# A planner that knows VectorE's delay between dependent neighbours, and convolution tiles one projection later, in a two-layer decoder trunk

## The chip, the core and the metric

The kernel runs on one NeuronCore of a Trainium2 chip. Its engines have their own instruction queues and meet by semaphores: TensorE (PE; its weight loads are PEld), VectorE (DVE), ScalarE (ACT), GpSimd (POOL) and SyncE (SP, which here only issues DMAs). The metric is the device time of one execution in microseconds, lower is better. Before the change it is 1433.64 us, the median of three runs from 1433.3 to 1433.87.

## What is computed

A causal decoder trunk of two layers on a sequence of 512 tokens with 1024 channels. Layer 0 mixes tokens by a gated linear recurrence and pooling, layer 1 by a conformer convolution module; behind either come cross-attention to 256 memory tokens and a gated feed-forward with a short convolution. The change touches the conformer's code and the scheduler of all. The conformer:

```python
def conformer_conv(x, norm, w1, b1, dw_w, dw_b, ln_g, ln_b, w2, b2):
    h = rms_norm(x, norm) @ w1 + b1
    h = jax.nn.glu(h, axis=-1)
    h = causal_dwconv(h, dw_w, dw_b)
    h = jax.nn.silu(layer_norm(h, ln_g, ln_b))
    return h @ w2 + b2

def layer(x, mem, ...):
    x = x + (mixer_ab(x, ...) if layer % 2 == 0 else conformer_conv(x, ...))
    x = x + cross_attn(x, mem, ...)
    return x + conv_ffn(x, ...)
```

All is float32. The depthwise convolution has 31 taps for each channel.

## The kernel before

Channels lie on the 128 partitions, tokens along the free dimension; the 1024 channels are 8 chunks of 128 x 512. A float32 product is made of three matmuls of rounded halves: the operand is split into a high part (ScalarE copies it to fp32r) and a low part (VectorE, or GpSimd, subtracts), and high x high, high x low, low x high are summed in PSUM (`mm3`). So one projection of a chunk is 8 x 3 = 24 matmuls of 512 columns, and every weight needs a ScalarE copy and a subtraction (in the profile wr<-wf and wr<-wf,wr).

**Who sets the order.** The kernel's code doesn't issue instructions. Every call makes a node in a `Recorder`, which notes what the node reads and writes; `run` (line 498 issues everything, so L498 is the line of nearly all rows) puts the nodes out in the order of `plan`. `plan` is a list scheduler: it walks through a modelled time; each engine, when it is free, takes the ready node that is due first (`late` computes the due times backwards from the end), but TensorE takes the ready node that was recorded first, up to 60 nodes ahead of its head (`PE_WINDOW`). The costs of nodes are a table in `cost` (line 271), DMAs among them. A node that depends on one of the same engine was ready as soon as that one's time had passed (`hop`, line 454); one on another engine 0.04 us after the end plus a latency. Buffers of PSUM are given out in order: five "mm", two "aux", one "stat". Each engine then runs its queue strictly in the order planned.

**The conformer** (`conformer`, line 1340). For each chunk c there are two projections, the gate (`gate`, followed by ScalarE's sigmoid) and the value (`gated`, where VectorE writes h = (value + bias) x sigmoid into one of three padded buffers). Of the 31 taps of the convolution, TensorE does the first 8 for chunks 0 to 6 and all for chunk 7 (`PE_GROUPS`): four DMAs on SP copy 32 channels each into four tiles with four shifts stacked (`stacked`, in the profile actf<-h), and `conv_pe` multiplies them by small tap matrices, in groups of four tiles that each fill 32 of the 128 output partitions (aux<-actf,wf; the shapes end in 512, 508 and so on). `conv` does the other taps of chunks 0 to 6: four on ScalarE and GpSimd, and 19 on VectorE, each of which adds to the aux tile what the tap makes of h (aux<-h,par,aux), so each depends on the one before it of the same chunk. `merge` then adds both parts and the bias on VectorE (actf<-aux,par,actf) and frees the aux buffer. After chunks 3 and 7 the sums over channels for the mean are taken on TensorE (`quarters`, stat<-actf,onesf); mean, variance and scale follow, and with the normalised chunks the output projections (pw2). To have matmuls for TensorE meanwhile, parts of the next cross-attention's work are recorded between: `mem.keys(n)` (24 matmuls of 256 columns each) and `mem.values` (48 matmuls of 512 each). The loop (line 1439) records for each c: gate projection of c+1, tiles of c, value projection of c+1, taps of c; behind the last chunk's tiles come the loads for the values.

Of the kernel before, what the change touches and what calls it, by code (L numbers as in the profile page):

```python
# [21 lines left out]
C = D // P  # L22
# [15 lines left out]
N_POOL = [4] * 7 + [0]  # L38
LAG = 5
PLAIN = 3  # L40

KE = 4
# [140 lines left out]
class Node:  # L183

    def __init__(self, index, eng):
        self.index, self.eng, self.calls, self.us, self.tail = index, eng, [], 0.0, 0.0
        self.table, self.port, self.lat = None, False, 0.0
        self.before, self.after = set(), set()
        self.start = self.end = None
# [11 lines left out]
class Recorder:  # L201
# [5 lines left out]
    WIRE = 0.83 / (256 * 1024)  # L207
    LAND = {"SP": 1.9, "ACT": 1.9, "POOL": 2.3}

    def __init__(self, tc):  # L210
# [36 lines left out]
    def touch(self, node, v, write):  # L247
        t = v.tile
        lo, hi, mask, _ = v.region()
        if t.psum:  # L250
            lo, hi, mask = 0, 127, 1
        if not t.nodes:
            self.tiles.append(t)
        if not t.nodes or t.nodes[-1] is not node:
            t.nodes.append(node)

        def meets(e):
            return e[0] <= hi and lo <= e[1] and e[2] & mask

        for e in t.writes + (t.reads if write else []):  # L260
            if meets(e) and e[3] is not node:
                node.before.add(e[3])
        if write:
            keep = lambda e: not (lo <= e[0] and e[1] <= hi and (e[2] & mask) == e[2])
            t.writes = [e for e in t.writes if keep(e)]
            t.reads = [e for e in t.reads if keep(e)]
            t.writes.append((lo, hi, mask, node))
        else:
            t.reads.append((lo, hi, mask, node))

    def cost(self, node, eng, method, args, how, reads):
        out = args[0]
        n = int(np.prod((reads[0] if not isinstance(out, View) else out).shape[1:]))
        if method == "dma_start":
            src = out if isinstance(out, View) else reads[0]
            node.tail += self.WIRE * 4 * n * src.shape[0] * (1.9 if "accum_op" in how else 1)
            window = any(k[0] == "window" for k in src.steps) or any(k[0] == "window" for r in reads for k in r.steps)
            node.us += 0.65 if window else {"SP": 0.42, "ACT": 0.42, "POOL": 0.6}[eng]
            return
        if eng == "PE":  # L280
# [3 lines left out]
            elif out.shape[0] == 32:  # L284
                node.us += 0.875 / 4
            else:
# [32 lines left out]
    def plan(self):  # L319
# [19 lines left out]
        def late(extra):  # L339
            for o in reversed(nodes):  # L340
                due = end if o.ideal is None else o.ideal + o.us
                for a in list(o.after) + extra.get(o, []):
                    due = min(due, a.due - self.HOP - o.lat - (o.tail + self.LAND[o.eng] + self.SAFE if o.tail else 0.0))
                o.due = due - 1.15 * o.us
# [51 lines left out]
        while done < len(nodes):  # L396
# [11 lines left out]
            for e, r in ready.items():  # L408
# [4 lines left out]
                for i, (_, _, o) in enumerate(r):  # L413
# [39 lines left out]
                    heapq.heappush(soon, (o.end, o.index, "end", o))  # L453
                    hop = lambda a: now + us if a.eng == o.eng and not o.tail else o.end + self.HOP
                    for a, at in [(a, hop(a)) for a in o.after] + [(a, now) for a in opens.get(o, [])]:
# [54 lines left out]
def trunk(ctx: ExitStack, tc: tile.TileContext, I: dict, out_t: bass.AP, out: bass.AP):  # L510
# [132 lines left out]
    class Norm:  # L643
        due = None
# [695 lines left out]
    def conformer(norm, nxt, mem, parked):  # L1340
# [97 lines left out]
        mu = stat_ps()  # L1438
        for c in range(C):
            if c < C - 1:  # L1440
                b = gate(c + 1, project(w[0], c + 1, norm.x))
                spread(c + 1)
            else:
                mem.keys(KE)
            conv_pe(c)
            if c < C - 1:
                gated(c + 1, b, project(w[1], c + 1, norm.x))
                if c < C - 2:
                    w = pieces(c + 2)
            else:  # L1450
                mem.eng = G
                ready = [mem.piece(i, park=True) for i in range(4)] + [mem.piece(i) for i in range(4, 8)]
            conv(c)
        merge(*pend.pop())
# [18 lines left out]
        mem.values(1, ready[4:])  # L1473
        for n in range(KE + 1, C):
            mem.keys(n)
# [128 lines left out]
```

## Time and profile before

| what | before |
|---|---|
| median of the runs | 1433.64 us (1433.3 to 1433.87) |
| the profiled execution's own time | 1433.83 us |
| its span, first to last instruction | 1432.0 us |
| PE busy | 1421.8 us |
| DVE busy | 1223.8 us, 1874 instructions |
| ACT busy | 853.2 us |
| POOL busy | 185.3 us |
| granted TensorE clock | 1.000 |

The profile is of one execution. Rows name an instruction by its engine, the line, and out<-in by the program's tiles (mm, aux, stat are PSUM; act, actf, wf, wr, tmp, h lie in SBUF). "x16" is a count. A time in brackets is the engine's idle time before the row and what ended it. The conformer stands between 735 and 925 us of the span, the two feed-forwards at about 350 to 735 and 1050 to 1425.

### The profile page before, as it was taken

To read this page: it belongs to the slowest core of one execution; us is meant where nothing else is said; L and a number is where in the kernel's file an instruction comes from. 1 tells how busy PE (TensorE), PEld (TensorE's weight loads), DVE (VectorE), ACT (ScalarE), POOL (GpSimd) and SP (SyncE) were. 2 spreads that over 40 slices of the span, in tenths; PEclk is the share of its full clock that TensorE was granted. 3 is DMA by queue.
4 is the path that set the end of the run, shared out by engine and by line. 5 is a ranking of instruction groups with operands and counts; after the bars stand their busy time and mean duration, and the time that the engine had idled before them with its cause. 6 is when DMAs were issued, how large, how long until landed. Compare 5 with 4: busy or idle time off the path is not lost. (4 is left out here: it accounts for less than half of the span.)

```text
span 1432.0 us, 20240 instructions
## 1 busy us (share of the span) xinstructions
PE 1421.8 (99%) x7512; PEld 1199.9 (84%) x7512; DVE 1223.8 (85%) x1874; ACT 853.2 (60%) x1298; POOL 185.3 (13%) x196
## 2 busy tenths in 40 slices
PE   9999999999999999999999999999999999999998
PEld 8888888888988888888886676888898888888888
DVE  8986964758999999999967996776699999999996
ACT  8578854446866566656643436654577665666654
POOL 0000000001111010110006663300011111011000
PEclk9999999999999999999999999999999999999999
DMA  9332322228877786886515572322688777787821
GB/s 349 104 103 74 123 96 90 76 86 224 234 205 209 208 215 188 216 211 178 166 57 136 134 230 75 118 84 79 175 230 213 205 192 221 205 222 181 216 90 60
DMA packets 75988, 231.91 MB, mean 162 GB/s; under 512 B 8561, under 2 KB 10609, under 8 KB 75889
## 3 DMA queue, kind: packets, MB, share of 16 engines
q1 hardware_dynamic: 61488, 192.20, 40.7%
q0 software_dynamic: 13824, 37.75, 15.6%
q8 instruction: 59, 0.97, 0.3%
q10 hardware_dynamic: 576, 0.67, 0.1%
q14 instruction: 41, 0.33, 0.1%
HBM read 207.52 MB, written 2.10 MB: 146 GB/s over the span
## 5 line engine op out<-in xcount | busy, mean ns | idle before, releaser
L498 PE MATMUL mm<-act,wr 128*128 128x512 f32 (+1 forms) x4599 | 987.3, 368 | 1.7 <-ACT tmp L498 1.0
L498 PEld LDWEIGHTS mm<-act,wr 128*128 128x128 f32 x4599 | 802.1, 188 | 155.2 <-issue 5.8
L498 ACT ACTIVATE wr<-wf 128x1024 fp32r<-128x1024 f32 x295 | 308.4, 1053 | 116.8 <-PE mm L498 27.0
L498 DVE TENSOR_TENSOR wr<-wf,wr 128x1024 fp32r<-128x1024 f32 x272 | 329.4, 1219 | 37.3 <-ACT wr L498 18.7
L498 PE MATMUL aux<-act,wr 128*128 128x512 f32 (+1 forms) x1509 | 293.7, 337 | 0.1
L498 PEld LDWEIGHTS aux<-act,wr 128*128 128x128 f32 x1509 | 232.6, 190 | 28.8 <-ACT tmp L498 0.5
L498 ACT ACTIVATE tmp<-aux 128x512 f32<-128x512 f32 (+1 forms) x189 | 107.5, 571 | 94.8 <-PE aux L498 93.6
L498 DVE TENSOR_TENSOR tmp<-tmp,tmp 128x512 f32<-128x512 f32 (+1 forms) x151 | 99.4, 658 | 10.1 <-ACT tmp L498 6.3
L498 POOL DMA_DIRECT2D wf<-in_wup x48 | 42.7, 889 | 500.9 <-ACT act L498 275.9
L498 DVE TENSOR_TENSOR x<-x,mm 128x512 f32<-128x512 f32 (+1 forms) x126 | 81.5, 648 | 22.3 <-PE mm L498 21.6
L498 DVE SCALAR_TENSOR_TENSOR aux<-h,par,aux 128x497 f32<-128x497 f32 (+18 forms) x133 | 93.1, 731 | 4.7 <-PE aux L498 2.1
L498 POOL DMA_DIRECT2D wf<-wf x48 | 41.5, 864 | 382.0 <-PE mm L498 129.7
L498 ACT ACTIVATE act<-tmp 128x512 fp32r<-128x512 f32 (+1 forms) x85 | 52.9, 627 | 59.5 <-DVE tmp L498 59.4
L498 ACT ACTIVATE act<-actf 128x512 fp32r<-128x512 f32 (+1 forms) x136 | 70.0, 536 | 28.4 <-DVE actf L498 26.4
L498 PE MATMUL aux<-act,act 128*128 128x256 f32 (+1 forms) x456 | 84.4, 327 | 0.0
L498 PEld LDWEIGHTS aux<-act,act 128*128 128x128 f32 x456 | 73.7, 189 | 11.4 <-ACT tmp L498 0.5
L498 DVE TENSOR_TENSOR act<-actf,act 128x512 fp32r<-128x512 f32 (+1 forms) x136 | 76.0, 583 | 1.7 <-ACT act L498 1.5
L498 DVE SCALAR_TENSOR_TENSOR tmp<-h,par,tmp 128x512 f32<-128x512 f32 x96 | 72.0, 750 | 5.3 <-ACT tmp L498 2.7
L498 ACT ACTIVATE tmp<-h,par 128x512 f32<-128x512 f32 (+3 forms) x69 | 52.6, 782 | 31.2 <-DVE h L498 30.9
L498 POOL TENSOR_TENSOR wr<-wf,wr 128x1024 fp32r<-128x1024 f32 x23 | 55.1, 2406 | 91.2 <-PE mm L498 42.2
L498 DVE TENSOR_TENSOR tmp<-mm,tmp 128x512 f32<-128x512 f32 x84 | 57.1, 685 | 6.4 <-PE mm L498 6.1
L498 DVE TENSOR_TENSOR act<-tmp,act 128x512 fp32r<-128x512 f32 (+1 forms) x85 | 57.6, 682 | 0.4 <-ACT act L498 0.2
(150 smaller groups left out, 1067.2 us busy)
## 6 DMA issues: line engine op xcount, KB each, us to landing
wf<-in_wup SPq DMA_DIRECT2D x144, 512.0 KB, 4.8
wf<-in_wup POOLq DMA_DIRECT2D x48, 512.0 KB, 5.7
wf<-in_wdown SPq DMA_DIRECT2D x48, 512.0 KB, 5.3
actf<-in_wup SPq DMA_DIRECT2D x48, 256.0 KB, 6.3
wf<-wf POOLq DMA_DIRECT2D x48, 256.0 KB, 6.0
wf<-in_pw SPq DMA_DIRECT2D x24, 512.0 KB, 4.0
wf<-in_win SPq DMA_DIRECT2D x20, 512.0 KB, 3.6
wf<-in_wk SPq DMA_DIRECT2D x16, 512.0 KB, 5.9
```

The lines of the kernel that those rows point to most:

```text
L498: getattr(eng, method)(*[real(a) for a in args], **{k: real(v) for k, v in how.items()})
```

## The change

It has three parts. The planner gets a delay (`DRAIN`): a node that reads what the node before it on VectorE (or ScalarE) wrote is ready 0.12 us (0.2 us) after that one's time, in the forward walk and in the due times. Costs are changed: a copy with stacked shifts takes SP 0.8 us rather than 0.65, and its bytes count twice; a convolution tile is 0.225 us, and 0.06 more in a first group. And the conformer's loop is written in half steps, one projection each, with the tiles and taps of a chunk `AFTER` = 2 half steps behind its own projection, which is behind the next chunk's whole projection; at the end one more block of keys (`mem.keys`) is recorded ahead of the last tiles.

```diff
+AFTER = 2
...
-        self.before, self.after = set(), set()
+        self.before, self.after, self.feeds = set(), set(), set()
...
+    DRAIN = {"DVE": 0.12, "ACT": 0.2}
...
                 node.before.add(e[3])
+                if not write:
+                    e[3].feeds.add(node)
...
-            node.us += 0.65 if window else {"SP": 0.42, "ACT": 0.42, "POOL": 0.6}[eng]
+            node.tail *= 2.0 if window else 1.0
+            node.us += 0.8 if window else {"SP": 0.42, "ACT": 0.42, "POOL": 0.6}[eng]
...
-                node.us += 0.875 / 4
+                node.us += 0.9 / 4 + (0.06 if how["start"] else 0.0)
...
-                    due = min(due, a.due - self.HOP - o.lat - (o.tail + self.LAND[o.eng] + self.SAFE if o.tail else 0.0))
+                    if a.eng == o.eng and not o.tail:
+                        due = min(due, a.due - self.DRAIN.get(o.eng, 0.0))
+                    else:
+                        due = min(due, a.due - self.HOP - o.lat - (o.tail + self.LAND[o.eng] + self.SAFE if o.tail else 0.0))
...
-                    hop = lambda a: now + us if a.eng == o.eng and not o.tail else o.end + self.HOP
+                    drain = self.DRAIN.get(o.eng, 0.0)
+                    same = lambda a: now + us + (drain if a in o.feeds else 0.0)
+                    hop = lambda a: same(a) if a.eng == o.eng and not o.tail else o.end + self.HOP
...
-        for c in range(C):
-            if c < C - 1:
-                b = gate(c + 1, project(w[0], c + 1, norm.x))
-                spread(c + 1)
+        for i in range(2 * C - 2 + AFTER):
+            c = i // 2 + 1
+            if i >= 2 * C - 2:
+                mem.keys(KE + i - 2 * C + 2)
+            elif i % 2 == 0:
+                b = gate(c, project(w[0], c, norm.x))
+                spread(c)
             else:
-                mem.keys(KE)
-            conv_pe(c)
-            if c < C - 1:
-                gated(c + 1, b, project(w[1], c + 1, norm.x))
-                if c < C - 2:
-                    w = pieces(c + 2)
-            else:
+                gated(c, b, project(w[1], c, norm.x))
+                if c < C - 1:
+                    w = pieces(c + 1)
+            if i == 2 * C - 2:
                 mem.eng = G
-                ready = [mem.piece(i, park=True) for i in range(4)] + [mem.piece(i) for i in range(4, 8)]
-            conv(c)
+                ready = [mem.piece(k, park=True) for k in range(4)] + [mem.piece(k) for k in range(4, 8)]
+            c = i + 1 - AFTER
+            if c >= 0 and c % 2 == 0:
+                conv_pe(c // 2)
+                conv(c // 2)
...
-        for n in range(KE + 1, C):
+        for n in range(KE + AFTER, C):
             mem.keys(n)
```

What this does to the queues is shown at three places. First TensorE around the tiles of chunk 1. Before (mm_7514 is the value projection of chunk 2, aux_7545 the convolution of chunk 1):

```order
L498 MATMUL mm_7514<-act_7308,wr_7116 128x512
L498 MATMUL mm_7514<-act_7298,wr_7346 128x512
L498 MATMUL aux_7545<-actf_7472,wf_7365 32x512
L498 MATMUL aux_7545<-actf_7482,wf_7365 32x512
L498 MATMUL aux_7545<-actf_7491,wf_7365 32x512
L498 MATMUL aux_7545<-actf_7499,wf_7365 32x512
L498 MATMUL aux_7545<-actf_7472,wf_7365 32x508
L498 MATMUL aux_7545<-actf_7482,wf_7365 32x508
L498 MATMUL aux_7545<-actf_7491,wf_7365 32x508
L498 MATMUL aux_7545<-actf_7499,wf_7365 32x508
L498 MATMUL mm_7514<-act_7310,wr_7116 128x512
L498 MATMUL mm_7514<-act_7320,wr_7116 128x512
```

And TensorE at the same place now (mm_7507 is the value projection of chunk 2, mm_7568 the gate of chunk 3):

```order
L508 MATMUL mm_7507<-act_7331,wr_7114 128x512
L508 MATMUL mm_7507<-act_7324,wr_7128 128x512
L508 MATMUL aux_7545<-actf_7450,wf_7354 32x512
L508 MATMUL aux_7545<-actf_7460,wf_7354 32x512
L508 MATMUL aux_7545<-actf_7469,wf_7354 32x512
L508 MATMUL aux_7545<-actf_7476,wf_7354 32x512
L508 MATMUL aux_7545<-actf_7450,wf_7354 32x508
L508 MATMUL aux_7545<-actf_7460,wf_7354 32x508
L508 MATMUL aux_7545<-actf_7469,wf_7354 32x508
L508 MATMUL aux_7545<-actf_7476,wf_7354 32x508
L508 MATMUL mm_7568<-act_7233,wr_7348 128x512
L508 MATMUL mm_7568<-act_7243,wr_7348 128x512
```

Before, the 8 tiles stood between matmul 18 and 19 of that projection; now all 24 are ahead of them.

Second VectorE at the taps of chunks 0 and 1. Before (aux_7435 and h_112 are chunk 0, aux_7545 and h_114 chunk 1, h_116 is the new h of chunk 2):

```order
L498 SCALAR_TENSOR_TENSOR aux_7435<-h_112,par,aux_7435 128x483
L498 SCALAR_TENSOR_TENSOR aux_7435<-h_112,par,aux_7435 128x482
L498 SCALAR_TENSOR_TENSOR aux_7545<-h_114,par,aux_7545 128x500
L498 SCALAR_TENSOR_TENSOR aux_7545<-h_114,par,aux_7545 128x499
L498 SCALAR_TENSOR_TENSOR h_116<-mm_7514,par,tmp_7518 128x512
L498 SCALAR_TENSOR_TENSOR aux_7545<-h_114,par,aux_7545 128x498
L498 SCALAR_TENSOR_TENSOR aux_7545<-h_114,par,aux_7545 128x497
L498 SCALAR_TENSOR_TENSOR aux_7545<-h_114,par,aux_7545 128x496
L498 SCALAR_TENSOR_TENSOR actf_7163<-aux_7435,par,actf_7163 128x512
L498 SCALAR_TENSOR_TENSOR aux_7545<-h_114,par,aux_7545 128x495
```

VectorE at these taps now (aux_7478 is chunk 0):

```order
L508 SCALAR_TENSOR_TENSOR h_116<-mm_7507,par,tmp_7513 128x512
L508 SCALAR_TENSOR_TENSOR aux_7478<-h_112,par,aux_7478 128x490
L508 SCALAR_TENSOR_TENSOR aux_7478<-h_112,par,aux_7478 128x489
L508 SCALAR_TENSOR_TENSOR aux_7545<-h_114,par,aux_7545 128x500
L508 SCALAR_TENSOR_TENSOR aux_7478<-h_112,par,aux_7478 128x488
L508 SCALAR_TENSOR_TENSOR aux_7545<-h_114,par,aux_7545 128x499
L508 SCALAR_TENSOR_TENSOR aux_7478<-h_112,par,aux_7478 128x487
L508 SCALAR_TENSOR_TENSOR aux_7545<-h_114,par,aux_7545 128x498
L508 SCALAR_TENSOR_TENSOR aux_7478<-h_112,par,aux_7478 128x486
L508 SCALAR_TENSOR_TENSOR aux_7545<-h_114,par,aux_7545 128x497
```

Taps of one chunk stood behind each other; now the taps of two chunks alternate, and so it goes on to chunk 6.

Third VectorE behind the LayerNorm's scale (aux_8500, then aux_8503), where the first normalised chunk (act) and the weights of the first three output projections (wr<-wf,wr) are made. Before:

```order
L498 TENSOR_TENSOR actf_7291<-actf_7291,aux_8500 128x512
L498 TENSOR_TENSOR actf_7480<-actf_7480,aux_8500 128x512
L498 SCALAR_TENSOR_TENSOR wr_8545<-mm_8160,rt,wr_8496 128x512
L498 SCALAR_TENSOR_TENSOR wr_8545<-mm_8340,rt,wr_8496 128x512
L498 TENSOR_TENSOR wr_8564<-wf_8472,wr_8540 128x1024
L498 TENSOR_TENSOR act_8576<-actf_8519,act_8553 128x512
L498 TENSOR_TENSOR act_8578<-actf_8559,act_8569 128x512
L498 TENSOR_TENSOR wr_8588<-wf_8503,wr_8574 128x1024
L498 TENSOR_TENSOR wr_8597<-wf_8510,wr_8590 128x1024
```

VectorE at that place now:

```order
L508 TENSOR_TENSOR actf_7495<-actf_7495,aux_8503 128x512
L508 TENSOR_TENSOR actf_7629<-actf_7629,aux_8503 128x512
L508 TENSOR_TENSOR actf_7631<-actf_7631,aux_8503 128x512
L508 TENSOR_TENSOR wr_8563<-wf_8445,wr_8505 128x1024
L508 SCALAR_TENSOR_TENSOR wr_8573<-mm_8237,rt,wr_8552 128x512
L508 TENSOR_TENSOR act_8577<-actf_8519,act_8558 128x512
L508 TENSOR_TENSOR wr_8583<-wf_8461,wr_8540 128x1024
L508 TENSOR_TENSOR wr_8595<-wf_8483,wr_8568 128x1024
```

Five chunks were scaled ahead of the first operand, and two value parts; now seven chunks and one value part. On TensorE the first three output projections ran two channel chunks of the first weight, then of the second and third; now they go through the three weights for one channel chunk after the other.

## The prediction

> **What bounds the kernel now.** The page comes first:
>
> ```profile
> span 1432.0 us, 20240 instructions
> PE 1421.8 (99%) x7512; PEld 1199.9 (84%) x7512; DVE 1223.8 (85%) x1874; ACT 853.2 (60%) x1298; POOL 185.3 (13%) x196
> ```
>
> TensorE is busy 1421.8 of 1432.0 us, and the change takes no matmul away. So only time in which TensorE waits can be won. The waits of PE, all of them:
>
> ```profile
> PE aux L498 <- DMA actf<-h: 1.6, 3, 1.0
> PE stat L498 <- POOL onesf L573: 1.0, 1, 1.0
> PE mm L498 <- ACT tmp L498: 1.0, 2, 0.5
> PE mm L498 <- DVE act L498: 0.6, 1, 0.6
> ```
>
> Read alone they leave little: 4.2 us, of which 1.6 belong to the convolution tiles (aux<-actf,wf), which wait for their shifted copies (actf<-h). But a matmul's end is modelled, so a wait can hide inside "busy". Starts are safer. Below, TensorE in seven stretches: each from the first tile of one chunk's convolution (chunks 0 to 6) to the next matmul that is no convolution tile, which starts where the stretch ends; the columns are the stretch, its length, the busy time of the tiles, clock, DMA share, GB/s.
>
> ```profile
> 759.14:761.35 2.21, 2.21 (x16) 1.00 0.00 0
> 772.47:774.32 1.85, 1.85 (x16) 1.00 0.09 38
> 784.10:789.38 5.28, 4.04 (x16) 1.00 0.79 258
> 801.85:803.70 1.85, 1.85 (x16) 1.00 0.13 53
> 814.84:818.06 3.22, 2.88 (x16) 1.00 0.59 188
> 828.71:830.53 1.82, 1.82 (x20) 1.00 0.93 369
> 843.01:845.68 2.67, 2.67 (x16) 1.00 0.87 324
> ```
>
> The same 8 tiles (two records each) take 1.85 us when nothing holds them, and 5.28, 3.22, 2.67 and 2.21 in chunks 2, 4, 6 and 0. The sum is 18.90 us against 7 x 1.85 = 12.95: **5.95 us** of waiting, not 1.6. [...]
>
> What the tiles of chunk 2 wait for stands in the DMA queue, TensorE and VectorE's own order:
>
> ```profile
> 777.89 0.75 DVE L498 SCALAR_TENSOR_TENSOR h<-mm,par,tmp 128x512 f32<-128x512 f32 x1
> 778.67 4.26 SPq L498 DMA_DIRECT2D actf<-h  x4
> 787.55 1.90 PE L498 MATMUL aux<-actf,wf 128*32 128x512 f32 x10 [0.98 <-DMA actf<-h]
> ```
>
> VectorE writes h at 777.89, four copies are issued over 4.26 us, and the last tile can go at 787.55: h to tiles is **9.7 us**. VectorE itself is the second bound of this stage, and in the middle of the feed-forward:
>
> ```profile
> 100.00:150.00 50.00, 50.00 (x222) 41.41 (x221) 38.31 (x57) 44.40 (x59) 0.23 (x2) 1.00 0.26 85
> 500.00:550.00 50.00, 49.52 (x259) 42.12 (x258) 48.28 (x72) 31.31 (x45) 6.10 (x7) 1.00 0.76 211
> 800.00:850.00 50.00, 49.67 (x244) 33.90 (x243) 49.01 (x74) 18.08 (x27) 30.49 (x22) 1.00 0.60 174
> ```
>
> After the stretch and its length come PE, PEld and DVE busy. From 800 to 850 VectorE is busy 49.01 of 50 us. The first row also gives the price of a 128x512 matmul that nothing disturbs: 50/222 = 0.225 us.
>
> **Part 1: tiles behind the next chunk's whole projection.** Before, 36 matmuls (chunk 2) or 42 (chunk 4) stand between the end of a chunk's projection and its tiles, which cut into the next chunk's second projection (the first order piece). Now 48 to 60 stand there, and the tiles of the chunk before: at least 48 x 0.225 + 1.85 = 12.7 us. Needed are the 9.7 us from h to tiles, which leaves 3.0 for an h that VectorE writes late; in the new order a merge and a tap stand right ahead of h, 1.3 us. So I count all 5.95 us as gone. If the cover fails (SP's queue holds the copies behind a weight load that waits for a free buffer), a chunk waits again, by 0.4 to 3.4 us as above. Chunk 7's tiles stood in two pieces, now in one:
>
> ```profile
> 789.38:801.85 12.47, 12.47 (x56) 1.00 0.59 161
> 827.82:828.71 0.89, 0.89 (x10) 1.00 0.95 348
> 858.15:860.84 2.69, 2.69 (x25) 1.00 0.28 105
> 864.03:868.29 4.26, 4.26 (x41) 1.00 0.00 0
> ```
>
> The first row holds 54 projection matmuls by the order: 12.47 - 54 x 0.225 = 0.3 us is what a switch between the two kinds costs. One switch fewer is 0 to 0.3; I take **0.2**.
>
> **Part 2: who is late next.** With two aux buffers, chunk c's tiles need chunk c-2 merged on VectorE. So VectorE's total has to fit. VectorE now:
>
> ```profile
> 764.33 13.66 DVE L498 SCALAR_TENSOR_TENSOR aux<-h,par,aux 128x497 f32<-128x497 f32 x18
> 793.36 3.90 DVE L498 SCALAR_TENSOR_TENSOR aux<-h,par,aux 128x484 f32<-128x484 f32 x6
> 797.16 0.75 DVE L498 SCALAR_TENSOR_TENSOR actf<-aux,par,actf 128x512 f32<-128x512 f32 x1
> ```
>
> 18 taps that each add to what the one before wrote: (777.89 - 764.33)/18 = **0.753 us** a tap. The six at 793.36 alternate between two chunks by the order: (797.16 - 793.36)/6 = **0.633**. The changed order has 21 dependent neighbours among its 133 taps, where there were 73. From chunk 0's first tap to chunk 6's merge that makes 112 x 0.633 + 21 x 0.753 + 13 x 0.66 (six h, seven merges) + 2.3 (one weight split, three key steps) = 97.6 us. TensorE's work beside it, from the end of chunk 0's tiles to the second sum for the mean: 321 matmuls x 0.225 + two key blocks at 3.1 + 6 x 1.85 + 6.95 (chunk 7) + 0.9 (first sum) + 8 switches x 0.3 = 99.8 us. They fit by 2 us, so the chain isn't slower than TensorE; but in the order a merge stands only two rows ahead of the next h, and the tiles that need it follow directly behind the projection that h needs. Seven such hand-overs at 0 to 0.2 us: **+0.5**, bounds 0 and 1.5. As it was, the last merge was early:
>
> ```profile
> 865.63 0.75 DVE L498 SCALAR_TENSOR_TENSOR actf<-aux,par,actf 128x512 f32<-128x512 f32 x1
> 874.14 2.48 DVE L498 TENSOR_TENSOR actf<-actf,aux 128x512 f32<-128x512 f32 x4 [6.51 <-PE aux L498]
> ```
>
> **Part 3: the LayerNorm and the first output projections.** Behind the spread scale, TensorE has 45 key matmuls to do and then needs the first normalised chunk and three weights:
>
> ```profile
> 888.47 5.95 PE L498 MATMUL mm<-wr,wr 128*128 128x256 f32 x45
> 894.26 0.39 PE L498 MATMUL mm<-act,wr 128*128 128x512 f32 x1
> 895.26 2.93 PE L498 MATMUL mm<-act,wr 128*128 128x512 f32 x11 [0.61 <-DVE act L498]
> 889.07 3.08 DVE L498 TENSOR_TENSOR actf<-actf,aux 128x512 f32<-128x512 f32 x5 [0.79 <-PE aux L498]
> 892.07 1.40 DVE L498 SCALAR_TENSOR_TENSOR wr<-mm,rt,wr 128x512 fp32r<-128x512 f32 x2
> 893.39 1.22 DVE L498 TENSOR_TENSOR wr<-wf,wr 128x1024 fp32r<-128x1024 f32 x1
> 894.52 1.29 DVE L498 TENSOR_TENSOR act<-actf,act 128x512 fp32r<-128x512 f32 x2
> ...
> 897.22 1.23 DVE L498 TENSOR_TENSOR wr<-wf,wr 128x1024 fp32r<-128x1024 f32 x1 [0.28 <-issue]
> ```
>
> Before, VectorE scales 5 chunks, splits two values and a weight, then the first operand (act), then the two other weights. Now it scales 7 at 0.60, one weight at 1.13, one value at 0.66, the operand at 0.62, two weights at 1.13. From 889.07 this puts the operand's end at 895.7 (was 895.2) and the third weight's at 898.0. TensorE starts at 894.26 and has 8 matmuls (1.8 us) to do before that third weight, where it had 14 (3.2) before 898.4 (the row at 897.22): it waits 2.0 us where it waited 1.0. So **+1.0**, bounds 0 (the scale arrives earlier against TensorE) and +2.2 (one key block, 3.1 us, has moved ahead of the chain, and 9 value matmuls, 2.0 us, behind its start, so that the cover shrinks by another 1.1).
>
> **Part 4: VectorE's order elsewhere.** Dependent neighbours on VectorE fall from 405 to 145 in the whole program, and at 0.12 us each it is relieved of some 30 us. That buys little, since TensorE hardly waits there; the two waits for ACT are
>
> ```profile
> 526.20 0.74 PE L498 MATMUL mm<-act,wr 128*128 128x512 f32 x2 [0.48 <-ACT tmp L498]
> ```
>
> and its twin in the second layer. TensorE's rows outside the conformer move by groups of 3 to 20. I take 0, bounds -1.0 (both waits go) and +3.0 (six such waits are added).
>
> **Sum**, against the profiled execution's own 1433.83 us (its span of 1432.0 and 1.8 around it): -5.95 - 0.2 + 0.5 + 1.0 + 0 = -4.65, 1429.2 us. The median of the runs is 0.2 below that execution, so **1429.0**. With all bounds on the good side -7.25, with all on the bad side about +0.8 (the copies covered, all else at its worst).
>
> **Rivals.**
> 1. *The waits only change their name.* The hand-overs of part 2 cost 1.5, part 3 2.2, part 4 another 1: -5.95 - 0.2 + 4.7 = -1.5, so 1432. For it: VectorE and TensorE are within 2 us over 100. Against it: the sums say that they fit. The same time comes if the copies are late again in one chunk (3.4 of the 5.95 was chunk 2 alone).
> 2. *Slower: alternating gains nothing, and VectorE becomes the bound.* If each tap took 0.753 whatever its neighbour, the 97.6 us would be 111.0, 11 above TensorE's work, and with only two buffers TensorE waits all of it: 1429 - 0.5 + 11.2 = 1440. It decides from 0.70 us a tap, where 112 x 0.067 uses up the 2 us of room and the gain. Against it: the six alternating taps at 0.633. [...]
> 3. *Slower: fillers.* A scheduler that sees the delay puts a 1.13 us weight split where 0.12 us of waiting stood, 49 times between the sum that reads PSUM and the one that needs it (66 such neighbours before, 17 after). If each held a buffer so long that TensorE waited the 0.48 of the row above, it would cost 23 us: 1452. It decides from 10 places. Against it: VectorE has no less total time than before, and TensorE's buffers (five mm, two aux) hid all but two such delays.
> 4. *The change doesn't do what it says*: excluded by the order, where both moves can be read.
>
> **How the numbers follow.** Forecast 0.76 (1426.4 to 1430.8), rival 1 0.16, rival 2 0.03, rival 3 0.05. Faster by over 0.2% (2.9 us, about what a measurement of this kernel can tell from none) is the forecast's case, below 1430.8; rival 1 is within 0.2%; 2 and 3 are slower. The range from 1426.0, just under all the good bounds together, to 1433.0, most of rival 1, leaves out the slow ones and the last part of rival 1.
>
> **What would show it.** In the profile after: the seven stretches of tiles at 1.85 each (part 1); no PE wait for DMA actf<-h; tap pitch 0.633 in alternation and VectorE's stretch from first tap to last merge near 98 us (part 2); a PE wait of 1.5 to 2.5 us in the first three output projections (part 3); still at most a few waits of 0.5 for ACT in the feed-forwards (part 4). Waits of PE for VectorE ahead of aux tiles beyond 2 us together, or more than four waits in the feed-forwards, would make it wrong.

## The result, and the profile after

The changed kernel takes 1423.95 us (median of five runs, 1423.58 to 1426.22) against 1433.6 before: a ratio of 0.9936, 95% interval 0.9922 to 0.995. The forecast was 1429.0 in a range from 1426.0 to 1433.0; the kernel gained 9.7 us where 4.6 were forecast. The profiled execution took 1423.58 us.

The page of the changed kernel, its span and first row:

```profile
span 1421.8 us, 20232 instructions
PE 1413.4 (99%) x7512; PEld 1198.6 (84%) x7512; DVE 1202.0 (85%) x1874; ACT 847.0 (60%) x1299; POOL 185.0 (13%) x196
```

VectorE does the same 1874 instructions in 21.8 us less. TensorE does the same 7512 matmuls and its busy time is 8.4 us less, at an unchanged clock: so most of what was won had been counted as "busy".

Where the time went shows best when both executions are cut at the same matmuls, the 1700th, 3400th, 4800th, 5300th and 7200th in TensorE's order. Each row is a stretch between two of them: its ends, its length, then PE, PEld, DVE, ACT and POOL busy with the number of instructions, clock, DMA share, GB/s. They are the start (layer 0's mixer and attention), the first feed-forward, the conformer and the second feed-forward; the second attention between the last two, 99.6 us in both, and the end behind them, the same in both, are left out. Before:

```profile
1.03:351.22 350.19, 350.19 (x1701) 296.46 (x1701) 260.71 (x410) 221.38 (x342) 8.49 (x33) 1.00 0.40 130
351.22:659.29 308.07, 307.48 (x1701) 266.86 (x1700) 300.28 (x451) 198.52 (x292) 35.58 (x41) 1.00 0.79 212
659.29:934.00 274.71, 272.53 (x1402) 209.57 (x1401) 225.56 (x332) 139.11 (x202) 99.05 (x68) 1.00 0.43 132
...
1033.57:1381.79 348.22, 347.62 (x1902) 300.87 (x1901) 337.46 (x510) 224.14 (x332) 39.04 (x45) 1.00 0.77 207
```

And after:

```profile
1.03:350.51 349.48, 349.32 (x1701) 295.20 (x1701) 258.63 (x410) 221.56 (x343) 7.51 (x32) 1.00 0.40 130
350.51:656.51 306.00, 306.00 (x1701) 267.25 (x1700) 294.88 (x451) 195.78 (x291) 36.34 (x42) 1.00 0.81 214
656.51:926.08 269.57, 268.09 (x1403) 208.74 (x1401) 217.96 (x332) 138.21 (x202) 99.13 (x68) 1.00 0.44 134
...
1025.66:1371.63 345.97, 345.97 (x1902) 301.21 (x1900) 331.78 (x510) 221.62 (x331) 38.93 (x45) 1.00 0.78 208
```

The conformer's stretch is 5.1 us shorter (274.71 to 269.57; the forecast was 4.65). The feed-forwards are 2.07 and 2.25 shorter and the start 0.7; there the forecast was 0. Together that is 10.2 us between these two executions; the medians differ by 9.7. In the first feed-forward PE was "busy" 307.48 us for work that now takes 306.00, so a wait of 1.5 us stood inside the busy column, and only 0.6 outside it.

One such place in the first feed-forward before. The columns are start, duration, and a group of TensorE's matmuls; the bracket is the idle time that the profile shows:

```profile
493.32 1.57 PE L498 MATMUL aux<-act,wr 128*128 128x256 f32 x8
494.95 1.31 PE L498 MATMUL mm<-act,wr 128*128 128x512 f32 x5
...
524.14 1.57 PE L498 MATMUL aux<-act,wr 128*128 128x256 f32 x8
526.20 1.57 PE L498 MATMUL mm<-act,wr 128*128 128x512 f32 x7 [0.48 <-ACT tmp L498]
```

The same two places after:

```profile
491.62 1.57 PE L508 MATMUL aux<-act,wr 128*128 128x256 f32 x8
493.04 1.55 PE L508 MATMUL mm<-act,wr 128*128 128x512 f32 x8
...
522.12 1.57 PE L508 MATMUL aux<-act,wr 128*128 128x256 f32 x8
523.53 1.55 PE L508 MATMUL mm<-act,wr 128*128 128x512 f32 x8
```

From the start of the same eight matmuls to the next group it was 1.63 and 2.06 us, and is 1.42 and 1.41. The first loss, 0.21, has no bracket at all; the second is 0.65 where the bracket says 0.48.

The waits of PE that the profile of the changed kernel lists:

```profile
PE mm L508 <- DVE act L508: 1.3, 1, 1.3
PE stat L508 <- POOL onesf L583: 1.0, 1, 1.0
PE aux L508 <- DVE wr L508: 0.2, 1, 0.2
```

No wait for the copies (DMA actf<-h), none for ScalarE, and none of an aux tile for a merge. The stretches of convolution tiles after, in the columns of the prediction: chunks 0, 2, 4 and 6, which had been held (1, 3 and 5 read 1.85, 1.85 and 1.83), and chunk 7 in one piece:

```profile
761.12:762.97 1.85, 1.85 (x16) 1.00 0.91 144
...
783.71:785.56 1.85, 1.85 (x16) 1.00 0.00 0
...
811.06:812.90 1.84, 1.84 (x16) 1.00 0.00 0
...
839.03:840.88 1.85, 1.85 (x16) 1.00 0.00 0
853.84:860.66 6.82, 6.82 (x64) 1.00 0.02 8
```

VectorE's taps in alternation, and the last chunk's taps where nothing is left to alternate with:

```profile
784.54 12.31 DVE L508 SCALAR_TENSOR_TENSOR aux<-h,par,aux 128x491 f32<-128x491 f32 x19
796.76 0.75 DVE L508 SCALAR_TENSOR_TENSOR actf<-aux,par,actf 128x512 f32<-128x512 f32 x1
...
854.61 6.06 DVE L508 SCALAR_TENSOR_TENSOR aux<-h,par,aux 128x489 f32<-128x489 f32 x8
860.58 0.42 DVE L508 TENSOR_TENSOR wr<-tmp,wr 128x256 fp32r<-128x256 f32 x1
```

(796.76 - 784.54)/19 = 0.643 us a tap in alternation, (860.58 - 854.61)/8 = 0.746 behind each other.

TensorE at the first output projections:

```profile
885.11 0.39 PE L508 MATMUL mm<-act,wr 128*128 128x512 f32 x1
886.81 1.63 PE L508 MATMUL mm<-act,wr 128*128 128x512 f32 x5 [1.31 <-DVE act L508]
888.28 0.63 PE L508 MATMUL aux<-act,wr 128*128 128x512 f32 x2
889.08 0.50 PE L508 MATMUL aux<-act,wr 128*128 128x512 f32 x1 [0.17 <-DVE wr L508]
```

By the starts it waits 1.70 - 0.225 = 1.48 and 0.80 - 0.45 = 0.35, together 1.8, where it waited 1.00 - 0.225 = 0.77 before.

### The profile page after: what moved, and what is told of

The parts are those of the page before. It is cut to its first block, busy times and chain, and to the rows that moved or that the text cites. A ratio compares the mean times of both kernels' runs of the same rounds, so it can differ in the third digit from the quotient of the medians.

```text
span 1421.8 us, 20232 instructions
## 1 busy us (share of the span) xinstructions
PE 1413.4 (99%) x7512; PEld 1198.6 (84%) x7512; DVE 1202.0 (85%) x1874; ACT 847.0 (60%) x1299; POOL 185.0 (13%) x196
## 4 chain that ended last, share of the span: by engine, by line
PE 98%; DVE 1%; DMA 1%; ACT 0%; issue 0%; SPq 0%; DVEq 0%
PE mm L508 70%; PE aux L508 27%; DMA wf<-in_mem 1%; PE stat L508 1%; DVE actf L508 0%; DVE wr L508 0%; ACT act L508 0%; DVE act L508 0%; ACT wf L508 0%; SPq L508 0%; DVE wf L508 0%; DVEq L1612 0%; ACT rtok L508 0%; DVE rtok L508 0%; DVEq L508 0%
## 5 line engine op out<-in xcount | busy, mean ns | idle before, releaser
L508 DVE SCALAR_TENSOR_TENSOR aux<-h,par,aux 128x500 f32<-128x500 f32 (+18 forms) x133 | 88.1, 727 | 3.9 <-PE aux L508 3.1
L508 ACT ACTIVATE tmp<-mm 128x512 f32<-128x512 f32 (+1 forms) x58 | 33.3, 574 | 55.7 <-PE mm L508 55.6
```

The lines of the kernel that those rows point to most:

```text
L508: getattr(eng, method)(*[real(a) for a in args], **{k: real(v) for k, v in how.items()})
```

## The experiments

Every run is compared with runs of the kernel before on the same chip (medians 1433.1 to 1433.4 in the sets below). "Dependents" are neighbours on VectorE of which the second reads what the first wrote, counted in the order; the number in brackets is those among the taps. Before it was 405 (73), after 145 (21).

### Which part of the change

First the four ways to take the change apart: the planner's delay, the cost table, the loop. e1 is the kernel before with the delay alone, e2 with the new loop alone, e3 the changed kernel without the delay, e4 the changed kernel with the old loop. The delay is these lines, present in e1 and e4 and absent from e2 and e3:

```diff
+    DRAIN = {"DVE": 0.12, "ACT": 0.2}
...
+                    if a.eng == o.eng and not o.tail:
+                        due = min(due, a.due - self.DRAIN.get(o.eng, 0.0))
...
+                    drain = self.DRAIN.get(o.eng, 0.0)
+                    same = lambda a: now + us + (drain if a in o.feeds else 0.0)
```

> Only the delay between dependent neighbours (DRAIN, forward and in the due times) is added to the kernel before; loop and costs stay as before. Theory A (the hidden waits of TensorE in the two feed-forwards, 2.1 us each by starts of matmuls, and 0.7 at the start came from a plan that took VectorE for faster than it is): both feed-forwards and the start gain as in the changed kernel, 5.0 us together, and the convolution tiles still wait for their copies by 4 to 6 us: 1428 to 1429. Theory B (the costs of DMAs or the loop moved those waits, and the delay only serves the conformer's taps): the feed-forwards stay as before, at most 1 us is gained, 1432.5 to 1433.6.

> Only the conformer's loop is changed (tiles behind the next chunk's whole projection); no DRAIN, old costs. Theory A: feed-forwards and start as before. In the conformer the waits for copies (5.95 us) go, but 81 of the 133 taps stand behind their own chunk's, so VectorE needs 97.6 + 60 x 0.12 = 104.8 us against TensorE's 99.8: TensorE waits some 3 to 5 us for merges instead: 1431 to 1433. Rival (VectorE isn't a bound there): the conformer gains its 5 us all the same, 1428.5.

> The changed kernel without DRAIN: new loop and new costs. Theory A: feed-forwards and start as before; in the conformer 67 dependent taps, VectorE 97.6 + 46 x 0.12 = 103.1 us against 99.8, so 2 to 4 of the 5.15 us gained there are lost to waits for merges: 1430.5 to 1432.5. Theory B: feed-forwards as in the changed kernel, total 1424 to 1426.

> The changed kernel with the old loop: DRAIN and new costs. With the costs of the stacked copies raised the planner may place the tiles later within its window of 60 matmuls. If the loop is what removes the copies' waits, 3 to 6 us of them stay and the time is 1427 to 1430 with the feed-forwards' 5 us gained; if the costs alone place the tiles well, 1424 to 1425.5.

Measured: e1 1423.7 us (ratio 0.9935, 0.9918 to 0.9951), e4 1424.51 (0.9937, 0.9923 to 0.9952), e3 1434.88 (1.0012, 1.0003 to 1.0021), e2 1436.19 (1.0021, 1.0011 to 1.0031). The delay alone is the whole gain. The loop adds nothing to it and loses a little without it. Neither theory for e1 foresaw that: the feed-forwards gained as A said, but the conformer did too. e2 and e3 took 2 to 3 us more than was expected of them.

Why the loop fails alone can be read in e3. Its seven stretches of tiles are as short as after (1.84 to 1.85), so the copies come in time, as Part 1 said. Chunk 2 of e3:

```profile
787.92:789.76 1.84, 1.84 (x16) 1.00 0.56 218
```

But TensorE now stands ahead of them, until VectorE has merged an older chunk and its aux buffer is free. TensorE's row at chunk 2 of e3:

```profile
787.92 1.49 PE L505 MATMUL aux<-actf,wf 128*32 128x512 f32 x12 [1.63 <-DVE actf L505]
```

And VectorE's merge that it waits for, behind ten taps:

```profile
780.58 6.43 DVE L505 SCALAR_TENSOR_TENSOR aux<-h,par,aux 128x486 f32<-128x486 f32 x10
786.92 0.74 DVE L505 SCALAR_TENSOR_TENSOR actf<-aux,par,actf 128x512 f32<-128x512 f32 x1
```

The waits of e3 ahead of aux tiles in the profile's list:

```profile
PE aux L505 <- issue: 3.5, 2, 1.8
PE aux L505 <- DVE actf L505: 1.6, 1, 1.6
```

They are 5.1 us, about what the copies had cost. The list names nobody for 3.5 of them ("issue"), but these two waits end at 818.50 and 845.80, each 0.1 us behind the end of a merge (818.40 and 845.70), so they are waits for merges too. That is the first rival of the prediction, the waits change their name; it comes true when the loop is changed and VectorE isn't relieved.

### Which engine's delay

e7 is the kernel before with the delay for VectorE alone (old loop, old costs), e8 with that for ScalarE alone:

```diff
-    DRAIN = {"DVE": 0.12, "ACT": 0.2}
+    DRAIN = {"DVE": 0.12}
```

> The delay alone (as in e1_drain_alone), for VectorE only: 155 dependent neighbours. If the gain is VectorE's, as in e1: 1423 to 1425. If ScalarE's 0.2 us had a part in the feed-forwards (ScalarE's copies free the mm buffers for which TensorE waited), 1 to 4 us of it are missing.

> The delay alone, for ScalarE only: 445 dependent neighbours on VectorE, 405 before. If the gain is VectorE's, as before or worse by up to 2 us: 1433 to 1436. If ScalarE's delay has a part in the feed-forwards, they gain 1 to 4 us.

e7 takes 1423.01 us (0.9926, 0.9912 to 0.9941), e8 1435.6 (1.0017, 1.0007 to 1.0026). ScalarE's delay has no part in the gain.

### Where VectorE's relief is worth something

e17 puts the delay only between two taps of one chunk, e18 between all other dependent neighbours (both in the planner's clock alone, so against e13 below):

```diff
+def is_tap(node):
+    method, args = node.calls[0][1:3]
+    return method == "scalar_tensor_tensor" and args[0].tile.psum and args[0].tile is args[3].tile
...
-  same = lambda a: now + us + (drain if a in o.feeds else 0.0)
+  same = lambda a: now + us + (drain if a in o.feeds and is_tap(o) and is_tap(a) else 0.0)
```

> The kernel before with 0.12 us in the planner's clock only between two taps of one chunk (VectorE's sums into an aux tile). Dependent neighbours by the order: 370, of them 36 among the taps. If the conformer's gain is the taps' alternation alone: conformer 268.8 to 269.6, feed-forwards 307.8 to 308.3 and 347.7 to 348.5 as before, 1427.5 to 1428.8. Rival (the relief of VectorE around the taps, at weight halves and LayerNorm, has a share): conformer 270.5 to 273, 1429 to 1432.

> The complement: the delay between all dependent neighbours on VectorE but two taps. Dependent neighbours: 212, of them 73 among the taps, as many as before. If the taps alone decide in the conformer: conformer 274 to 275.5 with the tiles held in three or four chunks, feed-forwards at 306.0 and 346.0, 1428 to 1429.5. Rival (relief around the taps suffices): conformer 269 to 272, 1423 to 1426.

e17 takes 1427.55 us (0.9961, 0.9947 to 0.9974), e18 1428.35 (0.9967, 0.9954 to 0.9979). The same stretches between matmuls as above, first feed-forward, conformer and second feed-forward, in e17:

```profile
350.43:658.43 308.00, 307.44 (x1701) 266.88 (x1700) 300.18 (x451) 198.39 (x292) 36.34 (x42) 1.00 0.80 212
658.43:927.21 268.78, 268.18 (x1403) 209.08 (x1402) 222.77 (x332) 138.91 (x202) 99.05 (x68) 1.00 0.45 135
...
1026.77:1374.74 347.97, 347.39 (x1901) 300.88 (x1900) 337.01 (x510) 224.11 (x332) 38.96 (x45) 1.00 0.77 207
```

And in e18:

```profile
351.03:657.06 306.03, 306.03 (x1702) 267.17 (x1700) 295.52 (x452) 199.32 (x292) 35.48 (x41) 1.00 0.81 213
657.06:931.38 274.32, 271.50 (x1402) 209.32 (x1401) 224.21 (x331) 138.66 (x202) 99.11 (x68) 1.00 0.45 133
...
1030.94:1376.94 346.00, 346.00 (x1901) 301.17 (x1900) 332.21 (x510) 225.19 (x332) 38.95 (x45) 1.00 0.78 208
```

This separates the gain by stage. With the taps alone the conformer falls by 5.9 us and the feed-forwards stay; with all but the taps the feed-forwards fall by 2.0 and 2.2 and the conformer stays. In e18 the tiles of chunks 2, 4 and 6 wait for copies as before (5.10, 3.40 and 2.30 us), in the old loop and with 73 dependents among the taps. Chunk 2:

```profile
781.54:786.64 5.10, 3.62 (x16) 1.00 0.80 264
```

In e17, with the same loop and 36 dependents, only chunk 1's stretch is longer than the least (2.47). Its h of chunk 2, and the tiles that need it:

```profile
775.51 0.75 DVE L512 SCALAR_TENSOR_TENSOR h<-mm,par,tmp 128x512 f32<-128x512 f32 x1 [0.37 <-PE mm L512]
784.85 1.92 PE L512 MATMUL aux<-actf,wf 128*32 128x512 f32 x16
```

From h to the tiles are 9.3 us here; before it was 6.2 (777.89 to 784.10). The time was gained at both ends. Before, VectorE began h of chunks 2, 4 and 6 by 2.1, 2.4 and 1.6 us after the end of its projection (the start of its last matmul and 0.227); in e17 by 0.3, 1.8 and 0.3. And by the order the planner places the tiles later: 42, 51 and 69 matmuls behind the projection, where it was 36, 42 and 42. So e17 shows that the loop isn't needed for the conformer's gain; it doesn't show that the place of the tiles had no part in it.

### What in the delay acts

The delay does two things: the planner's clock lets a dependent node wait, and the due times of a chain on one engine no longer count a hop and a latency at each step. Against e7, e13 has the clock half alone, e14 the due half alone:

```diff
e13
-                        due = min(due, a.due - self.DRAIN.get(o.eng, 0.0))
+                        due = min(due, a.due - self.HOP - o.lat)
e14
-                    drain = self.DRAIN.get(o.eng, 0.0)
+                    drain = 0.0
```

> The kernel before with the delay for VectorE (0.12 us) in the planner's clock alone; the due times count a hop and a latency for each step of a chain on one engine, as before. Dependent neighbours on VectorE by the order: 175 (35 among the taps). Theory A (the clock half is what acts: a dependent neighbour isn't ready when VectorE is, so another is taken): 1422.5 to 1424.5, feed-forwards at 306.0 and 346.0, conformer 269 to 270. Theory B (the due times have a share in the conformer): the feed-forwards at their floor, the conformer at 271 to 274, as in the runs of charge and preference: 1425 to 1428.

> The due times alone: a chain on one engine no longer counts a hop and a latency for each step (VectorE's counts 0.12), and the planner's clock has no delay. Dependent neighbours by the order: 417 (66 among the taps), as many as before. Theory A: no gain, 1432 to 1436, the feed-forwards at 308 and 348. Theory B: some of the conformer's 5 us, 1429 to 1431.

e13 takes 1422.81 us (0.9927, 0.9915 to 0.994), e14 1433.17 (0.9999, 0.999 to 1.0007): the clock half is all of it.

Then two kernels that take the clock half apart. e5 charges the 0.12 us to a dependent neighbour but leaves it ready at once; e6 charges nothing and takes another ready node where it can:

```diff
e5
+                    if e == "DVE":
+                        us += 0.12 if recent is not None and o in recent.feeds else 0.0
+                        recent = o
e6
+                if e == "DVE" and recent is not None:
+                    row.sort(key=lambda x: x[1][2] in recent.feeds)
```

> The kernel before, with a planner that adds 0.12 us to an instruction of VectorE whose neighbour ahead feeds it, but leaves it ready at once: it knows the time and has no reason to put another between (384 dependent neighbours, 405 before, 145 in the changed kernel). Theory R (relief: VectorE's work becomes shorter, which removes the waits): feed-forwards, start and conformer stay as before within 1.5 us, 1432 to 1435. Theory K (knowledge: the plan no longer counts on work that VectorE has not done, so that TensorE's order fits): the feed-forwards' and the start's 5 us are gained, and the waits for copies go, 1425 to 1429.

> The kernel before, with a planner that charges nothing for dependent neighbours but lets VectorE take another ready node first where there is one (212 dependent neighbours; among the taps 66, since the plan seldom has two chunks' taps ready). Theory R: the feed-forwards gain most of their 4.3 us, the conformer little (66 dependent taps against 73): 1428 to 1430.5. Theory K: the plan is as wrong as before and fillers come on top: 1433 to 1437.

e5 takes 1426.67 us (0.9951, 0.9937 to 0.9966) with 384 (51) dependents, e6 1427.94 (0.9961, 0.9946 to 0.9975) with 212 (66). In both the feed-forwards are at their floor (305.9 and 346.3, 306.1 and 346.0): either a planned VectorE as slow as the real one or a faster real one is enough there. In the conformer both fall short: e6 by held tiles (5.53 us in chunk 2, 3.17 in chunk 4), e5 by 2.0 us of waiting at the first output projections and a clock of 0.50 behind them (last section). e5's tiles are nearly free all the same (2.46 us in chunk 1, 2.07 in chunk 2, 1.82 to 1.85 in the others up to chunk 6), although VectorE is hardly relieved. Its h of chunk 6, and the tiles that need it:

```profile
831.64 0.74 DVE L503 SCALAR_TENSOR_TENSOR h<-mm,par,tmp 128x512 f32<-128x512 f32 x1
842.70 1.92 PE L503 MATMUL aux<-actf,wf 128*32 128x512 f32 x16
```

This h comes 7.6 us after its projection, later than before (1.6), but the tiles stand 69 matmuls behind that projection rather than 42, so the copies are there. Chunk 4 is alike: h 2.6 us after its projection (2.4 before), the tiles 51 matmuls behind it rather than 42, and no wait. So what frees these tiles is that the plan leaves the time that VectorE takes; an earlier h is not needed for it.

e15 gives e6 the due times as well, in case it had lacked those:

> VectorE takes a node that doesn't read what it has just written where it can, without time charged, as in the run that preferred, and now with the due times of the delay as well. Dependent neighbours by the order: 196 (56 among the taps). If the due times were what that run lacked: 1422.5 to 1424.5, conformer 269 to 270. If it lacked the time charged (a planned VectorE faster than the real one hands h over too late): as that run, 1426 to 1429, tiles held in two to four chunks.

It takes 1426.69 us (0.9953, 0.994 to 0.9965), with 56 dependents among the taps and tiles held in five chunks (3.01, 2.28, 2.90, 2.65, 2.55), as its second theory said. So the due times were not what e6 lacked.

Last the size, 0.03 and 0.24 us where 0.12 was:

> The kernel before with the planner's delay for dependent neighbours on VectorE alone, at 0.03 us rather than 0.12; loop and cost table as before. Dependent neighbours on VectorE by the order: 180 (42 of them among the taps), against 405 (73) before and 155 (29) with 0.12. Theory A (what is won is the size of the delay: the planner must both alternate and see the time that its dependent neighbours really take): the alternation comes, the knowledge doesn't, so it should be like the run that alternated and charged nothing: 1426 to 1429, with tiles of the convolution held in several chunks (5.5 and 3 us where 1.85 is the least) and the feed-forwards at their floor of 306.0 and 346.0. Theory B (any delay above zero sets the order, and the order is all): 1422 to 1424, all conformer tiles at 1.85 to 2.2, the conformer at 269.2.

> The same with the delay at 0.24 us, twice what the trace shows between dependent and independent taps. Dependent neighbours by the order: 145 (26 among the taps). Theory A (the size matters both ways): the planner now holds VectorE for slower than it is and places h and merges later than they come; TensorE's order is made for a slower VectorE, and 1 to 3 us come back in the conformer: 1424 to 1426. Theory B (only order counts; a few more alternations change little): 1422 to 1424, with no conformer tile held.

e9 takes 1423.25 us (0.9931, 0.9918 to 0.9945) with 180 (42) dependents, as good as 0.12, though one chunk's tiles are still held (3.71 us); theory A, that a quarter would alternate without gaining, was wrong. e10 takes 1426.14 (0.9953, 0.994 to 0.9965). The time is at the upper end of theory A's 1424 to 1426, but no tile is held, as theory B had said; in the execution that was traced (1428.82 us, the slowest of five) the first output projection waits 2.4 us with a clock of 0.50 behind it, and the second feed-forward has one wait of 1.05 us for ScalarE. So the number need not be right: in the old loop 0.03 does as well as 0.12, and 0.24 loses 3 us. Each is one plan, so whether the size or a chance of that plan loses them is not shown. Why a preference (e6, e15) leaves 56 to 66 dependent taps where a delay of 0.03 leaves 42 stays open.

### What was left over

After the change 1.8 us of waiting stay at the first output projections. e11 (on e7) moves two low halves of their weights to GpSimd, e12 also records all key blocks behind the values:

```diff
e11
-        w = [load_w(I["pw2"][n]) for n in range(3)]
+        w = [load_w(I["pw2"][n], G if n else None) for n in range(3)]
e12
-            else:
-                mem.keys(KE)
...
-        for n in range(KE + 1, C):
+        for n in range(KE, C):
```

> The delay on VectorE alone at 0.12, and the low halves of the second and third weight of the conformer's output projection are subtracted on GpSimd rather than VectorE. With the delay alone TensorE waits 1.06 + 0.35 us in the first output projections for VectorE, which makes three weights' low halves at 1.13 us among the normalised chunks. If that wait is what is left of part 3: it goes down to 0.2 to 0.5, 1421.9 (1421.4 to 1422.6) against 1423.0. Rival: GpSimd is slower with a 128x1024 tile or stands in VectorE's way, and the wait stays or grows: 1423 to 1425.

> As the run with the two halves on GpSimd, and the key blocks of the next attention are all recorded behind its values, none ahead of the last convolution tiles, so that more of TensorE's filler stands behind the LayerNorm's sums. If the cover in front of the first output projection is short, the rest of that wait goes too: 1421.0 to 1421.8. Rival: the last tiles come 3 us earlier on TensorE, ahead of the copies for chunk 7 or the merges, and a wait of 1 to 4 us appears there: 1422 to 1426.

e11 takes 1430.44 us (0.9981, 0.9972 to 0.999), 7 more than e7: the wait grew. TensorE's rows there:

```profile
886.36 0.50 PE L507 MATMUL mm<-act,wr 128*128 128x512 f32 x1 [1.06 <-ACT act L507]
891.61 2.50 PE L507 MATMUL mm<-act,wr 128*128 128x512 f32 x5 [4.75 <-DVE act L507]
```

VectorE's row of the first operand there, and GpSimd's row beside it:

```profile
888.71 2.84 DVE L507 TENSOR_TENSOR act<-actf,act 128x512 fp32r<-128x512 f32 x1
887.64 3.36 POOL L507 TENSOR_TENSOR wr<-wf,wr 128x1024 fp32r<-128x1024 f32 x1
```

The same operand in the changed kernel:

```profile
886.07 0.68 DVE L508 TENSOR_TENSOR act<-actf,act 128x512 fp32r<-128x512 f32 x1
```

TensorE needs it at about 885.3 in both. With two weights off VectorE, the planner put three small subtractions, a value's part and the first weight's low half ahead of it, so that VectorE came to it at 888.71 rather than 886.07. Then the operand took 2.84 us where it takes 0.68: it ended at 891.55, 0.55 us behind the weight's half that GpSimd was making (891.00). The trace of before has such a row as well: an operand of the same shape took 1.64 us at 904.22 and ended at 905.86, 0.55 behind GpSimd's subtraction (902.89 to 905.30). So the wait is another order on VectorE and, as the rival had said, GpSimd in VectorE's way; it came out larger than the rival's range. The clock of 0.51 from 890.20 to 897.10 (last section) is in the 7 us too. e12 takes 1424.27 us (0.994, 0.9928 to 0.9952), within its rival's range: no gain either.

e16 is the changed kernel with the small delay:

```diff
-    DRAIN = {"DVE": 0.12, "ACT": 0.2}
+    DRAIN = {"DVE": 0.03}
```

> The changed kernel with its delay at 0.03 us and for VectorE alone. The quarter delay in the old loop had one chunk's tiles held for copies (3.71 us where 1.85 is the least) and nearly no wait ahead of the output projections (0.16). If the loop gives the copies their time and the rest stays: all stretches at 1.85, the conformer at 267.5 to 268.3, 1421.0 to 1422.0. Rival: each plan has some 1 to 2 us of such waits at places that a small shift moves, and here they stand elsewhere: 1423 to 1425.

1424.65 us (0.9941, 0.9928 to 0.9955), so its rival held: its list of waits has 1.1 us ahead of aux tiles and 0.8 at the output projections, where e9's has 0.8 for copies and 0.3. The lowest median is e13's, 1422.81; its interval overlaps that of the changed kernel, so all that can be said is that the delay for VectorE in the planner's clock, alone, does no worse than the whole change.

## Why the prediction was wrong

**The step that failed is Part 4**, "I take 0, bounds -1.0 (both waits go) and +3.0". The two feed-forwards gave -4.3 us and the start -0.7, together -5.0. The relief was seen (260 fewer dependent neighbours), but its worth was read from the idle column, which shows two waits of 0.48. By starts, the first feed-forward lost 2.07 us and the second 2.25, in small places of which only the largest has a bracket. The prediction had warned of just this ("a wait can hide inside busy") and counted by starts in the conformer, then took the column elsewhere. A matmul of 512 columns is followed by the next after 0.227 us, one of 256 after 0.120 (medians). Against these the starts in the trace of before show five waits in the first feed-forward, 0.21, 0.15, 0.11, 0.23 and 0.65 (at 383.9, 419.2, 433.2, 494.5 and 525.3), where the column has 0.48. With them go seven neighbours that start 0.10 to 0.11 late, five of them right behind a wait: 2.11 together, all of the 2.07. In the second feed-forward it is 2.34 at 14 places; in the changed kernel no place is over 0.04. Four of the five waits end 0.05 us behind an instruction of ScalarE, one behind one of VectorE. How a VectorE that the plan takes for too fast makes ScalarE late there was not followed. e18 shows the term by itself: 4.3 us with the taps untouched; e5 and e6 show that a plan that knows VectorE's pace, or a faster VectorE, is enough. What the start's 0.7 is stays open; the start's length moved between 349.0 and 350.7 over the runs.

**Part 1** had the right size, but the loop isn't what brings it. Its 5.95 us went in full (seven stretches of 1.83 to 1.85), and chunk 7 went from 6.95 to 6.82 (0.13 for the 0.2). The prediction credited the loop, "tiles behind the next chunk's whole projection". e1, e7 and e13 win the same with the old loop, where the planner places most chunks' tiles later by itself once it takes VectorE for slower; e3 has the loop, and pays the 5 us at the merges. The mechanism, more work of TensorE between h and its tiles, was right: e5 frees chunks 4 and 6 by it alone. The 9.7 us from h to the tiles was real, and it left out that h itself came 1.6 to 2.4 us late in the three most held chunks.

**Part 2** held for the changed kernel: 21 dependent taps, alternation at 0.643 (forecast 0.633), and VectorE's stretch from the first tap to the last merge 763.11 to 861.66, 98.5 us (forecast 97.6), under TensorE's 99.8. The seven hand-overs cost 0, not 0.5. e3 shows that the loop needs this relief. That VectorE's total was the bound before is not shown. The same sum gives 103.8 us for the kernel before (60 x 0.633 + 73 x 0.753 + 8.6 + 2.3; the trace has 104.9), 4 over the 99.8. But e13, e17 and e5 have VectorE stretches of 103.1, 103.4 and 104.6 us, and none of their seven stretches of tiles is held by more than 0.62. The 99.8 belongs to the new order: between its first and its last tile stand 315 projection matmuls, in the kernel before and in e13 342.

**Part 3** held: +1.0 forecast, 1.8 - 0.77 = +1.05 measured, at the place named, though most of the wait (1.48) is for the first operand and only 0.35 for a weight.

**The rivals.** Rival 1 didn't happen in the changed kernel and did in e3. Rival 2 (alternating gains nothing) falls by the 0.643 of the taps: each lasts 12.31 - 18 x 0.643 = 0.73 us, so the next starts before it ends. Behind each other, each adding to what the one before wrote, they start 0.746 apart. Rival 3 (fillers) didn't show: no wait was added in the feed-forwards.

## What to carry to other kernels

Give a list scheduler the delay between dependent neighbours (here 0.746 us a tap against 0.643 in alternation), even a rough one: it costs a few lines, and it makes the planner interleave independent chains, which here took 22 us off VectorE, and place the other engines' work for the pace that VectorE really has. Price such a change by the starts of the bound engine over a whole stage, cut at the same instructions, not by its idle column. When a reader waits for a copy, look at both ends: how late the source was written, and how much work the plan has put between.

## What was unexpected in the hardware

In the traces of e2, e5, e10 and e11 the clock granted to TensorE fell to 0.50 at a short gap in the middle of dense work and came back after 3.41 or 6.83 us. Around the first output projections of e10, behind the stretch and the length, PE busy, clock, DMA share and GB/s:

```profile
885.00:887.60 2.60, 0.66 (x6) 0.99 0.31 76
887.60:894.40 6.80, 6.18 (x14) 0.50 0.33 125
```

And in e11:

```profile
890.20:897.10 6.90, 5.50 (x13) 0.51 0.06 23
```

And in e5:

```profile
889.17:892.58 3.41, 3.41 (x8) 0.50 0.53 210
```

In e10 and e11 the half clock lasts 6.83 us, and so it does in e2 at a wait of 3.9 us at chunk 4; in e5 it lasts 3.41. A matmul of 512 columns then takes 0.43 us rather than 0.225, so that the 14 of them that start in e10's half clock lose 2.8 us beside the wait itself.

The length of the gap alone doesn't tell where this happens. By the profile's lists the longest wait at the fall is 4.75 us in e11, 3.9 in e2, 2.4 in e10 and 1.4 in e5 (2.0 by starts, with those beside it); but e3's three waits ahead of aux tiles, of 1.6 to 1.8, each left the clock at 1.00 in the tiles behind them, as did the wait of 1.3 in the changed kernel at the first output projections. What decides it isn't shown. The five runs of e10 spread from 1424.57 (clock 0.999) to 1428.82 (0.996), by more than any other kernel here (0.6 to 3.1 us); that some of them had no half clock may be why, but with one trace for each kernel it isn't shown.
